# Moving the per-layer embedding from pairs 9 to 13 to pairs 2 to 6 of a mixture of experts, with 12 in place of 9 loads ahead of a branch

## The chip, the cores and the metric

The kernel runs on one core of one Trainium2 chip. The metric is the device time of one execution in microseconds (us); the time of a kernel is the median over its runs.

## What is computed

The program is two transformer blocks, one behind the other, on 512 tokens of width 1024, all in fp32. The second takes the first one's output. The change touches only the end of the first block:

```python
h = rmsnorm(x, g_ffn[i])
x = x + hier_moe(h, w_grp[i], w_exp[i], w1[i], w3[i], w2[i])
h = rmsnorm(x, g_ple[i])
x = x + jax.nn.sigmoid(h @ w_pg[i]) * (p[i] @ w_ple[i])
return rmsnorm(x, g_final)
```

`hier_moe` picks for every token one of 4 groups and two of its 8 experts, and adds for both `(silu(xb @ w1[e]) * (xb @ w3[e])) @ w2[e]`, weighted by the gates. An expert's w1 and w3 are 1024 x 512, its w2 is 512 x 1024. There is no limit to the tokens of an expert. The last but one line is the per-layer embedding: `p` is 512 x 256, `w_ple` 256 x 1024, `w_pg` 1024 x 1024. The product `p @ w_ple` depends on nothing that comes before it.

## The kernel before

**Order of the stages.** The first block's mixer, the experts, the embedding's gate (`w_pg`), then the second block's mixer and its MLP. The functions here are `moe` (L736 to L863), `Weights` (L686 to L733), `experts` (L1116 to L1270) and `Ple` (from L1274).

**Experts.** The 32 experts are worked through in 16 pairs, counted from 0. Each expert has room for 64 tokens, so that the two of a pair fill the two halves of 128 partitions. For a pair, `up` multiplies the gathered tokens by w1 and by w3 (`pa`, L1141 for one expert, L1142 for the other; 32 records each time), ScalarE (ACT) and VectorE (DVE) form the gated value `ms` (L1189 to L1191), TensorE (PE) transposes it (`pact`, L1204), ACT copies the transposes to `aT` (L1217), `second` multiplies by w2 (`py`, L1239 and L1240), ACT and DVE split the result into two parts `y`, and `back` multiplies by the dispatch matrix `OT` (`pc`, L1153), which DVE adds to the residual X (L1155). The pairs overlap: `up` with w1 of the next pair is issued ahead of the `py` of this one.

**Weights.** One pair needs 12 loads of 1 MB: four tiles each of w1, w3 and w2. `Weights` keeps a list of free slots. `next` gives the next tile and puts its slot back on the list, and `fetch` issues the load of a tile into a slot (L719, on SyncE, SP). All loads lie on the one queue of SP, which works in order, and each waits for one of eight semaphores, in turn, so that eight are outstanding. A load also waits for the readers of what lay in its slot. Of the slots, 8 are buffers of a ring (tiles `ww`), the others lie in other pools (`wr`, `we`, `wh`, `wm`, named after the pool).

**The embedding in steps.** `Ple.early` is a generator; `moe` calls its steps from hooks that `experts` runs behind `aT` of a given pair (L1218):

- At pair PLE_AT, `embed` (L826) takes 6 slots from the weights, two of pool `we` (for the result) and four of the ring. Then it loads p (`praw`, L1286, 0.5 MB) and w_ple (`wraw`, L1287, 1 MB) into ring buffers. Of 20 slots 14 are left.
- At the next pair p is transposed (8 transposes L1294) and split into two parts, w_ple too; at this and the following two pairs come 48 products `pw`.
- At PLE_AT + 4, `rest` (L830) gives the four ring buffers back: 18 slots.

```python
def embed():
    W.drop(tags[1:] + ring[:4])
    next(pl.steps)
...
steps = {PLE_AT + i: lambda: next(pl.steps, 0) for i in range(1, 4)}
steps.update({-1: where, PLE_AT: embed, PLE_AT + 4: rest})
xs, pa = experts(N, bufs, c, W, 0, 14, [d], then=steps, H=H)
```

**The branch.** Experts with more than 64 tokens are handled in a loop that runs only if there are any (L852). It stands between pairs 13 and 14. Ahead of it the kernel fetches AHEAD loads (L840) and reads the count into registers (L841) on all engines. With these inputs the loop is not entered. Behind it come the other weight loads, then the two halves of `w_pg`'s first part (`Ple.load`, L1306), g_final (L1335) and `w_pg`'s second part. The `w_pg` tiles are split for the products by ACT (L165) and DVE (L167), from `pl.start` at the end of pair 15.

**Who sets the order.** The code says what is computed; a scheduler of the framework orders the instructions of each engine when the kernel is built. Each engine then works through its own list in order.

Of the kernel before, what the change touches and what calls it, by code (L numbers as in the profile page):

```python
# [26 lines left out]
TMP = 5  # L27
LA = 0
LB = 1
PLE_AT = 9  # L30
AHEAD = 9
HI0 = 2048
NEG = -3.0e38

# [651 lines left out]
class Weights:  # L686
# [35 lines left out]
    def next(self):  # L722
        i, self.i = self.i, self.i + 1
        if i not in self.got:
            self.fetch(1, i)
        raw, slot = self.got.pop(i)
        self.free.append(slot)
        return raw
# [7 lines left out]
def moe(N, a, mg, mixed):  # L736
# [4 lines left out]
    with ExitStack() as ctx:  # L741
# [91 lines left out]
# [5 lines that stand above are left out]
        over = [s for s in W.free if s not in ring][-3:]  # L838
        W.drop(over)
        W.fetch(AHEAD)  # L840
        n = nc.values_load(more[:1, 0:1], min_val=0, max_val=7)  # L841
# [1005 lines left out]
```

## Time and profile before

| | |
|---|---|
| runs | 1790.24, 1790.33, 1791.94 us, median 1790.33 |
| profiled execution | 1791.52 us, its span 1789.7 |
| mean granted TensorE clock | 0.996 |
| TensorE busy | 1746.7 us, 98% of the span |
| VectorE, ScalarE busy | 857.4 us (48%), 578.6 us (32%) |
| moved by DMA | 322.60 MB, mean 180 GB/s |
| expert stage | about 400 to 850 us of the span |

Times of rows are microseconds from the start of the span. A row of a timeline gives an instruction's start and length, its engine and line, `out<-in` and, in brackets, the engine's idle time before it and what released it. Engine names with a q (SPq, PEq) are the sequencers, which issue the instructions. The clock is given as a share of 2.4 GHz.

### The profile page before, as it was taken

The numbers are of one execution on the slowest core, as the hardware profiler recorded it, in microseconds if no ns is written. First come the engines' busy times: TensorE is split into PE (matmuls) and PEld (weight loads), VectorE is DVE, ScalarE is ACT, GpSimd is POOL, SyncE is SP. The second block draws the span as 40 slices with busy tenths as digits, with TensorE's granted clock in tenths as the row PEclk, the third lists the DMA queues.
The fourth block names the chain that finished last, engine by engine and source line by source line (L and its number), as shares of the span: only waits on it lengthen the run. The fifth ranks groups of instructions, "written<-read, shape, count | busy, mean of one in ns | idle before, by whom it ended". The sixth has DMA issues, their size and how long they took to land.

```text
span 1789.7 us, 20888 instructions
## 1 busy us (share of the span) xinstructions
PE 1746.7 (98%) x8425; PEld 1236.4 (69%) x8425; DVE 857.4 (48%) x1604; ACT 578.6 (32%) x937; POOL 83.6 (5%) x144
## 2 busy tenths in 40 slices
PE   8999999999999998999999999999999999999998
PEld 6777888864444443443776678788888888888886
DVE  7665434465545544343855647544335433333333
ACT  5453322321111111211756742324223432222221
POOL 3001000110000000000020010000000000000000
PEclk9999999999999999999999999999999999999999
DMA  5123224879999999999211032112233133322221
GB/s 195 56 86 119 76 94 147 327 287 422 424 423 423 423 421 423 423 394 384 75 48 59 25 98 71 48 51 91 83 106 133 67 94 94 95 94 94 94 94 48
DMA packets 117888, 322.60 MB, mean 180 GB/s; under 512 B 8797, under 2 KB 69393, under 8 KB 93720
## 3 DMA queue, kind: packets, MB, share of 16 engines
q1 hardware_dynamic: 115176, 315.46, 46.3%
q0 software_dynamic: 2016, 3.64, 0.5%
q10 hardware_dynamic: 592, 2.10, 0.3%
q8 instruction: 68, 1.11, 0.3%
q14 instruction: 36, 0.29, 0.0%
HBM read 320.68 MB, written 4.19 MB: 182 GB/s over the span
## 4 chain that ended last, share of the span: by engine, by line
PE 51%; ACT 2%; DVE 1%; issue 1%; POOL 0%; DVEq 0%; POOLq 0%; ACTq 0%
PE acc L279 8%; PE acc L281 8%; PE acc L280 8%; PE pf L281 3%; PE pf L280 3%; PE pf L279 3%; PE pg L279 2%; PE pg L280 2%; PE pg L281 2%; PE psc L1671 2%; PE pu L279 1%; PE pu L280 1%; PE pu L281 1%; PE pa L1141 1%; PE py L1239 1%
## 5 line engine op out<-in xcount | busy, mean ns | idle before, releaser
L167 DVE TENSOR_TENSOR wlo<-wraw,whi 128x1024 fp32r<-128x1024 f32 (+2 forms) x165 | 225.8, 1380 | 368.8 <-PE pg L280 110.5
L165 ACT ACTIVATE whi<-wraw 128x1024 fp32r<-128x1024 f32 (+2 forms) x169 | 192.7, 1164 | 248.3 <-DMA wraw<-in_w_ff_dram 121.8
L279 PE MATMUL acc<-wh,whi 128*128 128x512 f32 (+1 forms) x432 | 164.1, 380 | 2.0 <-ACT sq L1462 1.2
L281 PE MATMUL acc<-wh,wlo 128*128 128x512 f32 (+1 forms) x432 | 163.6, 379 | 0.0
L280 PE MATMUL acc<-wh,whi 128*128 128x512 f32 (+1 forms) x432 | 163.4, 378 | 0.0
L279 PE MATMUL acc<-whi,wh 128*128 128x512 f32 x288 | 116.5, 405 | 1.5 <-ACT wh L165 1.5
L1155 DVE TENSOR_TENSOR X<-pc,X 128x512 f32<-128x512 f32 x128 | 79.6, 683 | 77.5 <-PE pc L1153 77.5
L280 PE MATMUL acc<-wlo,wh 128*128 128x512 f32 x288 | 115.4, 401 | 0.0
L281 PE MATMUL acc<-whi,wh 128*128 128x512 f32 x288 | 115.1, 401 | 0.1
L279 PE MATMUL pg<-wh,whi 128*128 128x512 f32 x256 | 101.4, 396 | 0.0
L281 PE MATMUL pg<-wh,wlo 128*128 128x512 f32 x256 | 101.3, 396 | 0.0
L280 PE MATMUL pg<-wh,whi 128*128 128x512 f32 x256 | 101.2, 395 | 0.0
L279 PE MATMUL pf<-whi,jh 128*128 128x512 f32 x256 | 101.1, 395 | 0.0
L280 PE MATMUL pf<-wlo,jh 128*128 128x512 f32 x256 | 101.1, 395 | 0.0
L281 PE MATMUL pf<-whi,jl 128*128 128x512 f32 x256 | 101.1, 395 | 0.0
L279 PEld LDWEIGHTS acc<-wh,whi 128*128 128x128 f32 x432 | 81.3, 188 | 21.1 <-ACT sq L1462 1.7
L281 PEld LDWEIGHTS acc<-wh,wlo 128*128 128x128 f32 x432 | 81.3, 188 | 17.2 <-issue 1.2
L280 PEld LDWEIGHTS acc<-wh,whi 128*128 128x128 f32 x432 | 81.3, 188 | 15.6
L1141 PE MATMUL pa<-ww,wm 128*64 128x512 f32 x176 | 79.3, 597 | 2.6 <-DVE y L169 2.2
L169 DVE SCALAR_TENSOR_TENSOR y<-py,gsl,y 128x512 fp32r<-128x512 f32 x32 | 24.0, 750 | 117.3 <-ACT y L165 116.6
L1142 PE MATMUL pa<-ww,wm 128*64 128x512 f32 x168 | 76.8, 598 | 0.0
L1153 PE MATMUL pc<-y,OT 128*128 128x512 f32 x256 | 69.4, 413 | 0.2 <-DVE X L1155 0.2
(484 smaller groups left out, 3468.7 us busy)
## 6 DMA issues: line engine op xcount, KB each, us to landing
ww<-in_w_dram SPq DMA_DIRECT2D x71, 1024.0 KB
wraw<-in_w_in_dram SPq DMA_DIRECT2D x44, 1024.0 KB
wr<-in_w_dram SPq DMA_DIRECT2D x34, 1024.0 KB
wm<-in_w_dram SPq DMA_DIRECT2D x33, 1024.0 KB
wraw<-in_w_ff_dram SPq DMA_DIRECT2D x32, 1024.0 KB
wh<-in_w_dram SPq DMA_DIRECT2D x31, 1024.0 KB
we<-in_w_dram SPq DMA_DIRECT2D x23, 1024.0 KB
wraw<-in_w_out_dram SPq DMA_DIRECT2D x8, 1024.0 KB
```

The costliest lines, as they stand in the source:

```text
L165: nc.scalar.activation(hi, src, AF.Copy, scale=scale)
L167: (pool or nc.vector).tensor_tensor(lo, src, f32v(hi), op=OP.subtract)
L169: nc.vector.scalar_tensor_tensor(lo, src, scale, f32v(hi), op0=OP.mult, op1=OP.subtract)
L279: mm(out, lhsT=lh, rhs=rh, start=start, stop=False, **kw)
L280: mm(out, lhsT=lh, rhs=rl, start=False, stop=False, **kw)
L281: self.mm = mm(out, lhsT=ll, rhs=rh, start=False, stop=stop, **kw).ins
L1141: nc.tensor.matmul(p[0:64], lhsT=x.xT[:, kk, :64], rhs=wt[0][:, k, :], start=kk == 0, stop=kk == 7)
L1142: x.ups.append(nc.tensor.matmul(p[64:128], lhsT=x.xT[:, kk, 64:], rhs=wt[1][:, k, :], start=kk == 0, stop=kk == 7).ins)
L1153: ins = nc.tensor.matmul(pc, lhsT=OT[:, t * P:(t + 1) * P], rhs=y[i], start=i == 0, stop=i == 1).ins
L1155: nc.vector.tensor_tensor(x, pc, x, op=OP.add)
L1239: nc.tensor.matmul(p[0:64], lhsT=aT[:, f, 0:64], rhs=wt[0][:, i, :], start=f == 0, stop=f == 3)
L1671: nc.tensor.matmul(pl[:, cs], lhsT=fk[:, m, cs], rhs=fq[:, m, cs], start=True, stop=True)
```

## The change

```diff
@@ -27,8 +27,8 @@
 TMP = 5
 LA = 0
 LB = 1
-PLE_AT = 9
-AHEAD = 9
+PLE_AT = 2
+AHEAD = 12
 HI0 = 2048
 NEG = -3.0e38
```

PLE_AT moves the embedding's steps from pairs 9 to 13 to pairs 2 to 6, and with them the time in which the weights have fewer slots. AHEAD puts three more loads in front of the branch.

On SP, in before, the loads of p and w_ple stand behind 120 weight loads:

```order
L719 DMA wm_4884<-in_w_dram 128x2048
L719 DMA ww<-in_w_dram 128x2048 x4
L719 DMA wr_4978<-in_w_dram 128x2048
L1286 DMA praw<-in_p_dram 128x4x256
L263 DMA wraw<-in_w_ple_dram 128x2x1024
L719 DMA wr_5027<-in_w_dram 128x2048
L719 DMA wr_5029<-in_w_dram 128x2048
```

and now behind 36, ahead of the tiles of w2 of pair 2:

```order
L719 DMA wm_3702<-in_w_dram 128x2048
L719 DMA ww<-in_w_dram 128x2048
L1286 DMA praw<-in_p_dram 128x4x256
L263 DMA wraw<-in_w_ple_dram 128x2x1024
L719 DMA wr_3753<-in_w_dram 128x2048
L719 DMA wr_3755<-in_w_dram 128x2048
```

Some loads further on SP, now, the last `ww` here is the second tile of w2 of pair 3:

```order
L719 DMA wh_3798<-in_w_dram 128x2048
L719 DMA ww<-in_w_dram 128x2048 x3
L719 DMA wm_3890<-in_w_dram 128x2048
L719 DMA wm_3892<-in_w_dram 128x2048
L719 DMA wm_3954<-in_w_dram 128x2048
L719 DMA wr_3966<-in_w_dram 128x2048
L719 DMA wr_3968<-in_w_dram 128x2048
L719 DMA wr_3987<-in_w_dram 128x2048
L719 DMA we_3989<-in_w_dram 128x2048
L719 DMA ww<-in_w_dram 128x2048
L719 DMA wh_3999<-in_w_dram 128x2048
```

It comes behind three `wr` and one `we`, which are needed later than it. In before a `ww` stands in the same way behind three `wr` and a `we`, at the tiles of w2 of pair 10.

On SP behind the branch (L841 ISA is its end), in before 11 weight loads stand ahead of w_pg:

```order
L841 ISA x2
L719 DMA wh_8942<-in_w_dram 128x2048
L719 DMA ww<-in_w_dram 128x2048 x5
L719 DMA wm_8987<-in_w_dram 128x2048
L719 DMA wm_9040<-in_w_dram 128x4x512
L719 DMA wm_9042<-in_w_dram 128x4x512
L719 DMA ww<-in_w_dram 128x4x512 x2
L263 DMA wraw<-in_w_pg_dram 128x4x512 x2
```

and now 8:

```order
L841 ISA x2
L719 DMA wr_8973<-in_w_dram 128x2048
L719 DMA ww<-in_w_dram 128x2048 x2
L719 DMA we_8987<-in_w_dram 128x2048
L719 DMA ww<-in_w_dram 128x4x512 x4
L263 DMA wraw<-in_w_pg_dram 128x4x512 x2
```

On ACT behind the branch, in before, the conversions of w_pg (`wh<-wraw`) begin behind the first `y` of pair 15:

```order
L852 UNCONDITIONAL_BRANCH x2
L1189 ACTIVATE ms<-pa,rsl 128x512
L1217 ACTIVATE aT<-pact 128x512
L165 ACTIVATE y<-py,gsl 128x512 x2
L1189 ACTIVATE ms<-pa,rsl 128x512
L1217 ACTIVATE aT<-pact 128x512
L165 ACTIVATE y<-py,gsl 128x512
L165 ACTIVATE wh_9120<-wraw 128x512
L195 ACTIVATE jk,ss<-X 128x512
```

and now four of them stand ahead of `aT` of pair 15, four more ahead of its `y`:

```order
L852 UNCONDITIONAL_BRANCH x2
L1189 ACTIVATE ms<-pa,rsl 128x512
L1217 ACTIVATE aT<-pact 128x512
L165 ACTIVATE y<-py,gsl 128x512 x2
L1189 ACTIVATE ms<-pa,rsl 128x512
L165 ACTIVATE wh_9120<-wraw 128x512 x4
L1217 ACTIVATE aT<-pact 128x512
L165 ACTIVATE wh_9201<-wraw 128x512 x4
```

## Rows read from the trace of the kernel before

**Rows 1.** The page, parts 1 and 2: engines, DMA tenths and GB/s in 40 slices.

```profile
PE 1746.7 (98%) x8425; PEld 1236.4 (69%) x8425; DVE 857.4 (48%) x1604; ACT 578.6 (32%) x937; POOL 83.6 (5%) x144
...
DMA  5123224879999999999211032112233133322221
GB/s 195 56 86 119 76 94 147 327 287 422 424 423 423 423 421 423 423 394 384 75 48 59 25 98 71 48 51 91 83 106 133 67 94 94 95 94 94 94 94 48
```

**Rows 2.** Stage table: us; busy (count) of PE, PEld, DVE, ACT, POOL; clock, DMA share, GB/s.

```profile
460.00:490.00 30.00, 30.00 (x147) 12.64 (x144) 15.88 (x47) 4.39 (x9) 1.98 (x2) 1.00 1.01 424
...
670.00:700.00 30.00, 22.94 (x101) 10.44 (x102) 13.72 (x29) 5.53 (x9) 1.06 (x1) 0.89 1.01 423
...
790.00:820.00 30.00, 28.47 (x127) 11.63 (x127) 14.46 (x28) 2.66 (x4) 0.00 (x0) 1.00 0.83 338
820.00:850.00 30.00, 27.44 (x116) 11.70 (x112) 11.24 (x18) 4.39 (x7) 0.00 (x0) 0.94 1.04 408
850.00:880.00 30.00, 29.98 (x141) 22.07 (x140) 27.88 (x56) 25.71 (x60) 3.40 (x4) 1.00 0.23 78
880.00:910.00 30.00, 28.56 (x131) 22.87 (x130) 21.55 (x45) 19.14 (x37) 2.98 (x6) 1.00 0.11 36
```

**Rows 3.** TensorE's timeline, pairs 2 and 3: start, us, line, out<-in, count.

```profile
466.97 0.59 PE L1239 MATMUL py<-ww,aT 128*64 128x512 f32 x1
...
480.94 2.12 PE L1153 MATMUL pc<-y,OT 128*128 128x512 f32 x8
...
493.61 0.59 PE L1239 MATMUL py<-ww,aT 128*64 128x512 f32 x1
```

**Rows 4.** TensorE's timeline, pairs 9 and 10; in brackets idle time before, releaser.

```profile
670.87 0.64 PE L1142 MATMUL pa<-wm,wm 128*64 128x512 f32 x1 [0.72 <-DMA wm<-in_w_dram]
...
695.02 1.11 PE L1239 MATMUL py<-ww,aT 128*64 128x512 f32 x1 [6.34 <-DMA ww<-in_w_dram]
...
699.28 0.59 PE L1239 MATMUL py<-ww,aT 128*64 128x512 f32 x1
...
699.71 0.59 PE L1239 MATMUL py<-ww,aT 128*64 128x512 f32 x1
```

**Rows 5.** SP's timeline (a DMA issue), then its waits, 660 to 710.

```profile
681.22 0.33 SPq L719 DMA_DIRECT2D ww<-in_w_dram  x1
...
SPq L719 <- PE pa L1142: 5.8, 2, 5.4
```

**Rows 6.** SP's timeline, pair 3: first issue's start, stretch of the x3 issues.

```profile
474.45 4.85 SPq L719 DMA_DIRECT2D wr<-in_w_dram  x3
```

**Rows 7.** The branch: timelines of TensorE and SP, line L852, DMA tenths 800 to 812.

```profile
807.51 0.59 PE L1141 MATMUL pa<-we,wm 128*64 128x512 f32 x1
807.52 0.59 PE L1142 MATMUL pa<-wh,wm 128*64 128x512 f32 x1
...
809.78 0.61 PE L1141 MATMUL pa<-ww,wm 128*64 128x512 f32 x1 [0.38 <-PEq L852]
...
786.83 20.36 SPq L719 DMA_DIRECT2D wh<-in_w_dram  x3
...
L852 SPq COMPARE_BRANCH  x1: 50/50/50, 793.5 to 793.5; - x1
...
L852 PEldq COMPARE_BRANCH  x1: 3366/3366/3366, 805.5 to 805.5; - x1
...
DMA  9978778555423211100001000090489999999999
```

**Rows 8.** Pair 15: timelines of TensorE, then ScalarE.

```profile
827.11 0.64 PE L1141 MATMUL pa<-ww,wm 128*64 128x512 f32 x1
...
834.13 2.14 PE L1153 MATMUL pc<-y,OT 128*128 128x512 f32 x8
838.83 0.84 PE L1204 MATMUL pact<-ident,ms 128*128 128x128 f32 x4 [2.56 <-DVE ms L1191]
839.32 3.59 PE L1153 MATMUL pc<-y,OT 128*128 128x512 f32 x8
842.84 0.64 PE L1239 MATMUL py<-wm,aT 128*64 128x512 f32 x1
...
839.70 0.60 ACT L1217 ACTIVATE aT<-pact 128x512 f32<-128x512 f32 x1 [2.94 <-PE pact L1204]
...
855.94 2.19 ACT L165 ACTIVATE wh<-wraw 128x512 fp32r<-128x512 f32 x4
```

## The prediction

> **What bounds the kernel now.** I read the page first, then the stage table, then the timelines of the engines around the places that the change touches. The page shows TensorE (PE) busy for 98% of the span, but also a band, slices 10 to 17, in which the DMA engines are full at 421 to 424 GB/s [rows 1]. That band is the expert stage, and the stage table narrows it: in every stretch that I read from 460 to 700 us the DMA share is 1.01, and only from 790 on does it fall [rows 2]. So between 430 and 790 us two things are nearly full at once. A pair of experts needs 12 loads of 1 MB; at 423 GB/s a load of 1.05 MB takes 2.48 us, so 12 take 29.8 us. TensorE needs less for a pair: it starts the products of one pair at 466.97 and of the next at 493.61, 26.6 us [rows 3]. The stream loses some 3 us of its lead per pair, and the kernel lives on the lead that it has at the start.
>
> Pairs are counted from 0, as in the code. The lead runs out at pairs 9 and 10. There TensorE waits twice for a load: 0.72 us and 6.34 us [rows 4]. The first is the lead at its end. The second is of another kind: the awaited `ww` was issued only at 681.22, after SP had waited up to 5.4 us for products (PE pa L1142) to release a ring buffer [rows 5]. It is the load that the embedding's 5 ring tiles push behind others. After that wait the granted clock is at its lower level: the five steps of products from 695.02 to 699.28 take 4.26 us, where five take 2.15 at the upper one (0.43 a step, 699.28 to 699.71) [rows 4]. The stage shows 0.89 for its mean clock [rows 2]. The three items sum to 0.72 + 6.34 + 2.1 = 9.2 us, and they are what moving the embedding could remove.
>
> **Part 1: the embedding at pairs 2 to 6.** Its own work (two loads, 8 transposes, 48 products, the splits) is the same instructions elsewhere: no term. What moves with it is the shortage of buffers: 20 weight slots become 14 for four pairs, then 18. Now the lead is largest there, so does a wait follow? The order shows one displaced load, the second tile of w2 of pair 3, behind four others. Its buffer comes free when the products with w3 of pair 3 end, 480.94 [rows 3]. A load on an idle queue takes about 4.5 us: when SP issues again at 806.86 (the last of its three `wh`, 786.83 + 20.36 - 0.33), the DMA engines are busy again from 808.4 on (slices of 0.3 us), then 2.48 for the bytes and something for completion [rows 7]. So it lands at about 485.5, and TensorE needs it at 493.61 [rows 3]: no wait, 8 us to spare. **The 9.2 us at pair 10 go.**
>
> But 14 slots hold less of a lead than 20, so the DMA engines, which ran without a pause before, now have some. Size: the displaced tile is now the 54th of the stream. SP keeps eight loads outstanding, so in before the 62nd was issued when the 54th had landed: 478.97 (the last of the three `wr`, 474.45 + 4.85 - 0.33) [rows 6]. Ahead of it there now lie p (0.5 MB) and w_ple (1 MB), 1.5 x 2.48 = 3.7 us: 482.7 if the queue never ran dry. It lands at 485.5 instead. **The stream is 2.8 us late**, call it 3. Bounds: 0 if the queue never runs dry; 8 if each of the four loads that are issued singly there cost its full 4.5 - 2.48 = 2 us. I take 3, since it comes from this place's own rows. From then on the queue is full as before, and a full queue can't catch up.
>
> What then is the 9.2 us worth? The last two loads that the branch needs, the second half of w1 of pair 15, are used at 807.51 and 807.52. Behind them SP had one more load, the last; its bytes stopped moving at 805.1 and SP resumed at 806.86, so the one before, 2.48 earlier, had landed between 802.6 and 804.4: I take 803.5, a lead of 4.0 us [rows 7]. TensorE comes 9 us earlier, waits for this same stream, and gets it 3 us later than before: 806.5 in place of 807.5. **Gain up to the branch: 1.0 us**, bounds +4.0 and -5.
>
> **Part 2: the branch.** In before, TensorE's sequencer reaches the branch at 805.5 and takes 3.37 us in it, while queued products run to 809.4: a gap of only 0.38 [rows 7]. Now the sequencer stands at products that wait for a load until 806.5; behind them only four steps are left. In before 809.78 - 805.5 - 3.37 = 0.9 us lie around those 3.37; 806.5 + 3.4 + 0.9 gives a restart at 810.8, where it was 809.78: **+1.0 us**. Bounds: -1 if the branch stays hidden, +4.5 if the code's fetch takes twice as long beside full DMA engines (in before they are idle then).
>
> **Part 3: 12 loads ahead, and who waits behind them.** SP can't pass the branch before all its loads have landed: it stood at the three `wh` for 20.36 us, and the DMA engines were idle until its next issue [rows 7]. With three more loads (7.5 us) and a stream 3 us late it resumes at 806.86 + 10.5 = 817.4. Behind it now come 8 weight loads, then w_pg, where 11 came before. The first four, w3 of pair 15, land by 817.4 + 4.5 + 3 x 2.57 = 829.6; their second half is needed in the middle between 827.11 and 834.13 [rows 8], plus the 1.0: no wait, by some 2 us. The first half of w_pg lands at 817.4 + 4.5 + 8 x 2.57 = 842.5 (1.05 MB at the 408 GB/s of 820 to 850 [rows 2]); as the queue has been some 1 us slower than its mean at other places, 842.5 to 843.5.
>
> Who waits for it is new. On ScalarE (ACT) the four conversions of this load stood behind the `y` of pair 15; the order now puts them ahead of `aT` of pair 15. In before `aT` runs at 839.70, 0.9 us after its transposes, and the products start at 842.84 [rows 8]. Now: 843 + 4 conversions, 2.2 us (four in 2.19 [rows 8]) + `aT` 0.6 + 0.3 = 846.1 to 846.6, and DVE's two subtractions of the same load stand ahead of its adds in the same way. **+3.7 us at the last products, which takes in part 2.** Bounds: +1.0 if w_pg lands by 840; +5.5 if the adds hold the matrix products back too.
>
> The Trainium skill (TensorE: Matmul & The Clock Gate, Engine queue depths) calls ACT and DVE strict FIFO. By that the `aT` must wait and the sum is this one; without it the sum would end with part 2, at +1.0. No row of before shows an instruction there that overtakes another.
>
> **Part 4: the clock.** After the 2.56 us wait at 838.83 eight matrix products take 3.59 us, where eight take 2.14 [rows 8]: the lower level already costs 1.5 there. TensorE will now wait some 4 us more right behind. After 6.34 us it cost 2.1 [rows 4]; part of it will lie inside the wait. I take **+1.0**, bounds 0 and 3.4. The same page's Terms put the penalty at throttled time x (1 - K/N), half of the time at the lower level; by that the sum would be higher by another 1, the row says less because part of that time is idle.
>
> **Part 5: given back.** The conversions are done earlier, but TensorE is busy 29.98 of the 30 us after 850; only 880 to 910 has 1.4 us of idle time [rows 2]. **-0.3**, bounds 0 and -1.4.
>
> **Sum:** +3.7 + 1.0 - 0.3 = +4.4 us. The profiled execution took 1791.52; its sum is 1795.9. The median of three runs, 1790.33, lies 1.2 lower, so for the median 1794.7; I say **1795**.
>
> **Rivals.** *The gain is kept* (faster): the stall goes and the stream has room to follow, so that all 9.2 us stay; 1790.3 - 9.2 = 1781. It needs 9 us of slack in the stream, and the lead at the branch was 4.0. A smaller version, no lost lead (+4.0) and `aT` not held, ends at about 1786. Together **0.10**.
>
> *Nothing is left of it* (no change): the stream is the limit before and after, the 9.2 us turn into a wait at pair 14 or 15, and w_pg lands by 840 or the wait for it is shared with the pause that is there already (2.56 us). Then -1 to +2: 1790 to 1792. **0.33**.
>
> *More than I count* (slower still): the stall comes back at pair 3. The point from which it decides is 8 us of delay of one load, the price 6 to 9 us taken from a stretch where the lead then still grows, so much of it would be hidden. **0.04** within the slower case.
>
> **Chances.** A measurement of this kernel tells about 0.2% (3.6 us) from no change: 1786.7 to 1793.9. Forecast and what is slower than it by the bounds of parts 2 to 4: **0.57** slower; **0.33** the same; **0.10** faster. The range takes in the no-change case to its lower half and the upper bounds (+5.5 + 3.4 + 1 = about +10): **1788.5 to 1800**. The forecast's own range is 1793 to 1800.
>
> **What would show it.** No DMA wait above 2 us between 430 and 780, and pairs of 26.6 to 28 us wherever the embedding has no work; a new wait of about 6 us for a load of w1 of pair 15 at 793 to 800, with the clock down after it; PE's branch gap above 2 us; SP's longest wait at L852 ending at about 817; `aT` of pair 15 behind four `wh<-wraw` at about 845 to 847. I am wrong if DMA share drops nowhere in 455 to 490, if the last `py` starts before 844, or if the restart behind the branch is before 809.

## The result, and the profile after

The changed kernel takes 1801.21 us in the median of 5 runs (1800.26 to 1801.98), the kernel before 1790.33 (1790.16 to 1792.42). Run against run the ratio is 1.0053, with a 95% interval of 1.0042 to 1.0064: 9.5 us slower (7.5 to 11.5). The profiled execution took 1801.21 us, its span is 1799.3, 9.6 more than before; the mean granted clock is 0.994. The direction is the one forecast. The size is twice the forecast 4.7, the median lies 1.2 us above the upper end of the range (1800), and the loss comes from another place than the one that was to carry most of it.

The stage table of the kernel after, same columns as in [rows 2]:

```profile
430.00:460.00 30.00, 30.00 (x151) 13.11 (x152) 17.16 (x45) 5.28 (x11) 0.99 (x1) 1.00 1.00 404
460.00:490.00 30.00, 30.00 (x145) 12.33 (x142) 16.33 (x51) 4.81 (x11) 1.98 (x2) 1.00 0.95 376
...
550.00:580.00 30.00, 29.27 (x126) 13.43 (x125) 9.33 (x22) 4.57 (x8) 0.87 (x1) 1.00 1.00 403
670.00:700.00 30.00, 29.27 (x141) 13.09 (x141) 15.83 (x39) 4.20 (x9) 1.06 (x1) 1.00 1.01 422
790.00:820.00 30.00, 19.53 (x57) 6.96 (x55) 9.50 (x19) 2.06 (x3) 0.00 (x0) 0.77 0.88 368
```

Two stretches of the kernel before that were not shown ahead, for comparison:

```profile
430.00:460.00 30.00, 30.00 (x151) 12.83 (x151) 17.16 (x48) 5.25 (x12) 0.99 (x1) 1.00 1.01 423
...
550.00:580.00 30.00, 29.27 (x143) 12.78 (x141) 13.84 (x36) 4.02 (x8) 1.06 (x1) 1.00 1.01 423
```

What was to go is gone: at 670 to 700 TensorE is busy for 29.27 us in place of 22.94, at the full clock. What was feared is there too. The DMA engines moved 404, 376 and 403 GB/s at 430 to 460, 460 to 490 and 550 to 580, where they moved 423 to 424: 19, 48 and 20 GB/s less for 30 us each, 2.6 MB, or 6.2 us of a stream of 423 GB/s. And nearly all of the loss is in one stretch, 790 to 820: TensorE is busy for 19.53 us of 30 (28.47 before), with a mean clock of 0.77.

TensorE's timeline of the kernel after in that stretch and at pair 15:

```profile
801.21 1.97 PE L1141 MATMUL pa<-ww,wm 128*64 128x512 f32 x2 [4.67 <-DMA ww<-in_w_dram]
804.21 1.11 PE L1142 MATMUL pa<-ww,wm 128*64 128x512 f32 x1 [1.03 <-DMA ww<-in_w_dram]
...
809.38 0.79 PE L1142 MATMUL pa<-ww,wm 128*64 128x512 f32 x1
...
810.44 0.59 PE L1142 MATMUL pa<-wm,wm 128*64 128x512 f32 x1
...
816.87 1.08 PE L1141 MATMUL pa<-ww,wm 128*64 128x512 f32 x1 [4.55 <-PEq L852]
...
817.75 1.06 PE L1141 MATMUL pa<-ww,wm 128*64 128x512 f32 x1
...
820.17 0.59 PE L1141 MATMUL pa<-ww,wm 128*64 128x512 f32 x1
...
847.44 1.11 PE L1204 MATMUL pact<-ident,ms 128*128 128x128 f32 x4 [2.57 <-DVE ms L1191]
...
851.40 0.64 PE L1239 MATMUL py<-ww,aT 128*64 128x512 f32 x1
```

SP's timeline of the kernel after around the branch (the issues of the three `wr` reach over it):

```profile
795.56 25.11 SPq L719 DMA_DIRECT2D wr<-in_w_dram  x3
820.78 0.85 SPq L719 DMA_DIRECT2D ww<-in_w_dram  x2
```

Line L852 of the kernel after (ns as min/median/max, first and last start):

```profile
L852 PEldq COMPARE_BRANCH  x1: 6146/6146/6146, 810.4 to 810.4; - x1
```

DMA tenths of the kernel after from 800 to 820, 40 slices of 0.5 us:

```profile
DMA  8999999989999999999999999998898632310000
```

SP's waits at the branch, for its eight semaphores (first and last start), of the kernel after, then of the kernel before:

```profile
L852 SPq EVENT_SEMAPHORE  x8: 17/17/17, 809.8 to 819.9; - x8
L852 SPq EVENT_SEMAPHORE  x8: 17/17/17, 803.5 to 806.4; - x8
```

TensorE stood at w1 of pair 15 for 4.67 and 1.03 us, and took its last tile (L1142, `wm`) at 810.44, where it took it at 807.52 before [rows 7]. SP passes the first of its waits there 6.3 us later than before (809.8 and 803.5), which agrees with the 6.2 us of the stream. The row of that last tile shows no wait: after the 4.67 us its clock is at the lower level, and the six steps from 804.21 to 809.38 take 5.17 us, 0.86 each, where a step at the upper level takes 0.43 [rows 4]. So about the last 0.6 us of the delay before the branch (810.44 less 809.8) are the clock's.

TensorE's sequencer reached the branch at 810.4, 4.9 us later than before (805.5), and stayed in it for 6.15 us in place of 3.37. TensorE restarts at 816.87 in place of 809.78: **+7.1 us**, 4.9 + 2.8 less 0.6 that lay around the branch before and no longer does. SP issues again at 820.78 (the forecast had 817.4), where it was 806.86. The DMA engines, nearly idle beside the branch before [rows 7], are at 8 tenths or more until 815.5 now.

Then the clock is down: the step from 816.87 to 817.75 takes 0.88 where one at the upper level takes 0.43 [rows 4], and the four steps up to 820.17 take 3.3 us in place of 1.7, some 1.6 more. The last products start at 851.40 in place of 842.84 [rows 8], +8.6. The remaining microsecond of the 9.6 lies behind, and I did not locate it.

ACT's timeline of the kernel after at pair 15:

```profile
846.85 2.19 ACT L165 ACTIVATE wh<-wraw 128x512 fp32r<-128x512 f32 x4 [1.48 <-DMA wraw<-in_w_pg_dram]
848.95 0.57 ACT L1217 ACTIVATE aT<-pact 128x512 f32<-128x512 f32 x1
```

The conversions of w_pg do stand ahead of `aT`, as in the order, and ACT waits 1.48 us for the load. But TensorE's transposes (`pact`) come only at 847.44, and `aT` at 848.95. From the transposes to the last products it is 4.0 us as before (851.40 - 847.44 here, 842.84 - 838.83 in [rows 8]): this wait costs nothing here.

### The profile page after: what moved, and what is told of

Read it like the earlier page. It is cut to its first block, busy times and chain, and to the rows that moved or that the text cites. A ratio compares the mean times of both kernels' runs of the same rounds, so it can differ in the third digit from the quotient of the medians.

```text
span 1799.3 us, 20889 instructions
## 1 busy us (share of the span) xinstructions
PE 1752.2 (97%) x8425; PEld 1237.9 (69%) x8425; DVE 858.0 (48%) x1604; ACT 578.6 (32%) x937; POOL 83.5 (5%) x144
## 4 chain that ended last, share of the span: by engine, by line
PE 50%; ACT 2%; DVE 2%; issue 1%; POOL 0%; DVEq 0%; POOLq 0%; ACTq 0%
PE acc L279 8%; PE acc L281 8%; PE acc L280 8%; PE pf L281 3%; PE pf L280 3%; PE pf L279 3%; PE pg L281 2%; PE pg L279 2%; PE pg L280 2%; PE psc L1671 2%; PE pu L281 1%; PE pu L279 1%; PE pu L280 1%; PE pa L1141 1%; PE py L1239 1%
## 5 line engine op out<-in xcount | busy, mean ns | idle before, releaser
L1142 PE MATMUL pa<-ww,wm 128*64 128x512 f32 x232 | 109.4, 617 | 1.5 <-DMA ww<-in_w_dram 1.5
L1141 PE MATMUL pa<-ww,wm 128*64 128x512 f32 x152 | 74.4, 634 | 10.7 <-DMA ww<-in_w_dram 4.7
```

Source lines behind the costliest of these rows:

```text
L1141: nc.tensor.matmul(p[0:64], lhsT=x.xT[:, kk, :64], rhs=wt[0][:, k, :], start=kk == 0, stop=kk == 7)
L1142: x.ups.append(nc.tensor.matmul(p[64:128], lhsT=x.xT[:, kk, 64:], rhs=wt[1][:, k, :], start=kk == 0, stop=kk == 7).ins)
```

## The experiments

Two questions were open. Is the branch's length a matter of the DMA engines? And is the late stream a matter of the slots? All ratios are against runs of the kernel before on the same chip.

**1. The embedding early, 9 loads ahead.**

```diff
-PLE_AT = 9
+PLE_AT = 2
 AHEAD = 9
```

> The embedding at pairs 2 to 6 as in the change, but 9 loads ahead of the branch as before. Theory A (the branch's code fetch queues behind the weight loads that are still on the DMA engines): the stream is as late as in the change (TensorE waits for w1 of pair 15 until about 801, reaches the branch at about 810.4), but hardly a load is left beside the fetch, so the branch takes 3.4 to 4.5 us in place of 6.15 and the restart comes at 814 to 815.2; the time is 1.7 to 2.8 us below the changed kernel's, 1797 to 1799 for a before of 1790. Rival B (6.15 us is what a branch costs that TensorE reaches with nothing queued, whatever the DMA engines do): 6.1 us, restart 816.9, time as the change, 1800 to 1801. Rival C (the conversions of w_pg ahead of aT cost 3 us, as the prediction had it): they stand behind aT here, so more than 3 us below the change even with a branch of 6 us.

1796.39 us, ratio 1.0024 (1.0015 to 1.0034). Line L852 of this run, then the restart in TensorE's timeline:

```profile
L852 PEldq COMPARE_BRANCH  x1: 3352/3352/3352, 809.8 to 809.8; - x1
```

```profile
813.50 0.78 PE L1141 MATMUL pa<-ww,wm 128*64 128x512 f32 x1 [2.34 <-PEq L852]
```

TensorE reaches the branch at 809.8, 0.6 us before the change does, and is through in 3.35 us: theory A, and not B. Three loads less beside the branch are worth 3.4 us at the restart (813.50 against 816.87), those 0.6 and 2.8 of the branch. Rival C's 3 us are not there: from the restart to the last products it takes 34.7 us in this run (they start at 848.25) and 34.5 in the change. But by the ratios the time is some 5 us below the change's, where theory A had 1.7 to 2.8; the rest of it lies behind pair 15 and was not located.

**2. The embedding late, 12 loads ahead.**

```diff
 PLE_AT = 9
-AHEAD = 9
+AHEAD = 12
```

> The embedding at pairs 9 to 13 as before, but 12 loads ahead of the branch. Theory A: nothing changes up to the branch (stall of 6.3 us at pair 10, branch reached at 805.5), then the fetch queues behind three loads and the branch takes about 6 us: restart at about 812, 2 to 3 us later than before; the conversions of w_pg stand ahead of aT but w_pg lands by 840. Time 2 to 4 us above before, 1792 to 1794. Rival B (the branch's length does not depend on the DMA engines): 3.4 us, restart 809.8, no change, 1789.5 to 1791.

1796.54 us, ratio 1.0026 (1.0016 to 1.0036), a little more than theory A had. Line L852 of this run:

```profile
L852 PEldq COMPARE_BRANCH  x1: 4832/4832/4832, 805.8 to 805.8; - x1
```

TensorE's timeline of this run, restart and pair 15, then ACT's:

```profile
811.16 0.61 PE L1141 MATMUL pa<-ww,wm 128*64 128x512 f32 x1 [1.54 <-DVEq L852]
...
840.20 0.66 PE L1204 MATMUL pact<-ident,ms 128*128 128x128 f32 x4 [2.57 <-DVE ms L1191]
...
846.14 1.11 PE L1153 MATMUL pc<-y,OT 128*128 128x512 f32 x2 [3.89 <-ACT aT L1217]
847.18 1.12 PE L1239 MATMUL py<-wm,aT 128*64 128x512 f32 x1
```

```profile
843.41 2.19 ACT L165 ACTIVATE wh<-wraw 128x512 fp32r<-128x512 f32 x4 [5.29 <-DMA wraw<-in_w_pg_dram]
845.51 0.57 ACT L1217 ACTIVATE aT<-pact 128x512 f32<-128x512 f32 x1
```

The branch takes 4.83 us with the embedding where it was, so it is the loads beside it that lengthen it. That is only 1.4 us at the restart (811.16 against 809.78). The larger part stands at pair 15: here TensorE is early enough for part 3 of the prediction. ACT waits for w_pg until 843.41, converts for 2.2 us, and `aT` follows at 845.51; TensorE waits 3.89 us for it, and the last products start at 847.18, 4.3 us later than before. My expectation said that w_pg would land by 840; that was wrong, and with it the size.

**3. The embedding at pairs 5 to 9, 9 loads ahead** (`PLE_AT = 5`).

> The embedding at pairs 5 to 9, 9 loads ahead. Theory: the loss of the stream comes from having 14 slots while the lead is long; at pair 5 the lead is still some 20 us, so a walk through the queue by hand has the DMA engines idle once for about 5 us around 572 and TensorE waiting some 2 to 3 us at pair 6, the last loads of w1 of pair 15 5 us later than before, and a branch of 3.4 to 4.5 us: 1795 to 1799. Rival (the loss is made by pairs 2 to 4 alone): a stream on time, 1789 to 1791.

1797.98 us, ratio 1.0035 (1.0020 to 1.0049). Stage table of this run, then TensorE's timeline:

```profile
550.00:580.00 30.00, 27.34 (x130) 11.93 (x128) 17.16 (x39) 6.90 (x11) 1.06 (x1) 1.00 0.78 319
```

```profile
579.26 0.64 PE L1240 MATMUL py<-ww,aT 128*64 128x512 f32 x1 [1.94 <-DMA ww<-in_w_dram]
...
814.10 0.61 PE L1141 MATMUL pa<-ww,wm 128*64 128x512 f32 x1 [2.09 <-PEq L852]
```

The stream pauses at the new place, 319 GB/s in place of 423, 7.4 us; TensorE waits for the displaced load there, and the restart is at 814.10. It reaches the branch at 810.4, just when the change does, and with 9 loads ahead takes 3.37 us there. The pairs 2 to 4 are no exception.

**4. The embedding at pairs 7 to 11, 9 loads ahead** (`PLE_AT = 7`).

> The embedding at pairs 7 to 11, 9 loads ahead. Theory: here 14 slots hold the lead that is left, so the DMA engines do not run dry, and the displaced load is still early enough (a wait of 1 to 2 us in place of 6.3 at pair 8). The stream is on time, TensorE waits about 2 us for w1 of pair 15 and reaches the branch at about 805, the restart is at 809 to 809.8: most of the 9.2 us that go at pair 10 are lost to the stream and to the branch, -1 to +0.5 us, 1789 to 1791. Rival (the stream has room): 4 to 9 us faster, 1781 to 1786.

1791.57 us, ratio 0.9997 (0.9987 to 1.0006). Stage table of this run, then TensorE's timeline:

```profile
550.00:580.00 30.00, 29.27 (x142) 12.88 (x139) 13.84 (x36) 4.03 (x8) 1.06 (x1) 1.00 1.01 423
```

```profile
804.83 0.64 PE L1142 MATMUL pa<-ww,wm 128*64 128x512 f32 x1 [1.74 <-SPq L852]
...
809.61 1.08 PE L1141 MATMUL pa<-wr,wm 128*64 128x512 f32 x1 [2.85 <-PEq L852]
```

With the lead down to what 14 slots can hold, the stream does not pause. The stall of 6.34 us is gone, and the time is the same: TensorE waits 1.74 us for the second half of w1 of pair 15 instead (the row names SP at L852; SP stands there for the same loads, one after the other from 804.8 on, when TensorE goes on), and 2.85 us at the branch, which is no longer hidden. That is 4.2 of the 9.2 us, with the 0.38 at the branch before taken off. At the transposes of pair 13 TensorE is 5.4 us ahead of the kernel before (782.59 against 788.03), so the other 3.8 are lost ahead of it; I did not take them apart in this run.

**5. Late, 12 loads ahead, conversions behind.** As experiment 2, and with the conversions of w_pg on ACT, and DVE's subtractions of the same load, held behind `aT` of pair 15:

```diff
-        nc.scalar.activation(aT, pt.rearrange("p (f s) -> p f s", f=4), AF.Copy)
+        turned = nc.scalar.activation(aT, pt.rearrange("p (f s) -> p f s", f=4), AF.Copy).ins
...
-                    then.get(pi + 1, int)()
+                    with tc.issue_after(turned):
+                        then.get(pi + 1, int)()
```

> As the run with the embedding late and 12 loads ahead, but the conversions of w_pg are held behind aT of pair 15 on ACT and behind the adds on DVE. Theory: there aT waited for them and for the w_pg load (3.89 us on TensorE behind aT, last products 4.3 us later than before, of which 1.4 from the branch); with them behind, the last products start at about 844.2 and only the branch's 1.4 us and a little are left: 0.5 to 2.5 us above before. Rival (the wait is for w_pg's bytes, whatever the order): as that run, 4 to 5.5 us above before.

1792.89 us, ratio 1.0006 (0.9996 to 1.0015). TensorE's timeline of this run:

```profile
840.58 0.66 PE L1204 MATMUL pact<-ident,ms 128*128 128x128 f32 x4 [2.58 <-DVE ms L1191]
...
843.01 0.64 PE L1239 MATMUL py<-wm,aT 128*64 128x512 f32 x1
```

From the transposes to the last products it is 2.4 us, and the wait for `aT` is gone. The last products start 4.2 us earlier than in experiment 2 (843.01 against 847.18), though the restart is 0.4 later: that is what the order cost there. That the time is level with before is in part the clock: the branch still takes 5.05 us and the restart is 1.8 us later than before (811.54), but the eight products behind the transposes take 2.09 us in place of 3.59 [rows 8], at a mean clock from 820 to 850 of 1.00 in place of 0.94 [rows 2]. Why the clock did not fall here was not tested.

**6. The change, conversions behind.** The same edit on the changed kernel.

> The change with the conversions of w_pg held behind aT of pair 15. Theory: in the change the restart behind the branch is so late (816.9) that w_pg has landed by then and aT waits 0.6 us for the conversions at most; so no difference: within 1 us of the change, 9 to 11 us above before. Rival (the prediction's part 3: this order is the main loss): 3 us or more below the change.

1800.82 us, ratio 1.0046 (1.0029 to 1.0062), which overlaps the change's own. TensorE's timeline of this run:

```profile
815.77 1.08 PE L1141 MATMUL pa<-ww,wm 128*64 128x512 f32 x1 [5.01 <-PEq L852]
...
851.10 1.12 PE L1239 MATMUL py<-ww,aT 128*64 128x512 f32 x1
```

The gap at the branch is there (5.01 us), and the last products start at 851.10, where they start at 851.40 in the change. The edit that took 4.2 us off experiment 2 brings the change 0.3 us there, and no gain in time that four runs can tell.

**7. Only the slots.** The embedding late and 9 loads ahead, as before; six slots are withheld from pair 2 to pair 6, and no other work is moved. (The change gives four of its six back at pair 6, here it is all six.)

```diff
+        held = tags[1:] + ring[:4]
+        steps[2] = lambda: W.drop(held)
+        steps[6] = lambda: W.free.extend(held)
         xs, pa = experts(N, bufs, c, W, 0, 14, [d], then=steps, H=H)
```

> The kernel before with the embedding where it was, at pairs 9 to 13, and 9 loads ahead; only the six weight slots are taken away at pair 2 and given back at pair 6, with no load or product moved. Theory (14 slots at a long lead make the DMA engines run dry): the DMA share falls below 1 between 450 and 490, the stream is 4 to 6 us late from then on, the lead ends one or two pairs earlier, the last load of w1 of pair 15 lands at 808 to 810 and the restart is 4 to 5 us later than before: 4 to 6.5 us above before. Rival (the lateness comes from the 1.5 MB of p and w_ple going first): the DMA share stays at 1.01, within 1 us of before.

1798.07 us, ratio 1.0031 (1.0019 to 1.0044). Stage table of this run, then TensorE's timeline (this kernel's lines are three higher, L1144 is L1141):

```profile
430.00:460.00 30.00, 30.00 (x151) 12.81 (x151) 17.17 (x48) 5.09 (x12) 0.99 (x1) 1.00 0.91 355
460.00:490.00 30.00, 30.00 (x147) 12.62 (x143) 15.78 (x47) 4.46 (x10) 1.98 (x2) 1.00 0.97 395
```

```profile
817.00 0.61 PE L1144 MATMUL pa<-wr,wm 128*64 128x512 f32 x1 [0.31 <-PEq L855]
```

355 and 395 GB/s in place of 423 and 424: 2.9 MB, 6.9 us, without p or w_ple in the stream at that place. So the slots by themselves make the stream late. All of the loss lies ahead of 490 here; from 550 to 580 this run moves 423 GB/s, so the change's 20 GB/s less there are not explained by it. The restart is at 817.00, 7.2 us late (4 to 5 were expected), and the branch is hidden but for 0.31 us. TensorE met the late loads at pairs 9 and 10, with seven waits of 0.36 to 1.28 us between 643 and 701: at the transposes of pair 10 it is 6.0 us later than before (689.18 against 683.19). The rest came in among the embedding's products, and I did not take it apart.

**8. The embedding at pairs 8 to 12, 9 loads ahead** (`PLE_AT = 8`).

> The embedding at pairs 8 to 12, 9 loads ahead. A walk through the queue finds no pause of the DMA engines and no wait of TensorE for a displaced load, and the stream on time: TensorE reaches the branch 1 to 2 us earlier than before and the restart is at 807.8 to 809.5: 0 to 2 us below before. Rival (a gain of the whole 9 us): 6 us or more below.

1791.29 us, ratio 0.9997 (0.9987 to 1.0007). TensorE's waits in this run from 430 to 790 (us in total, times, longest), then in the kernel before:

```profile
PE pa L1141 <- DVE y L169: 6.5, 9, 0.7
PE pw L279 <- ACT we L1304: 2.7, 4, 0.7
```

```profile
PE pa L1141 <- DVE y L169: 5.1, 7, 0.7
```

TensorE's timeline of this run around pairs 9 and 10, and the restart:

```profile
659.20 0.64 PE L1239 MATMUL py<-wh,aT 128*64 128x512 f32 x1
...
673.70 1.02 PE L1142 MATMUL pa<-ww,wm 128*64 128x512 f32 x2
...
675.31 1.07 PE L1141 MATMUL pa<-ww,wm 128*64 128x512 f32 x2
...
765.31 0.59 PE L1239 MATMUL py<-ww,aT 128*64 128x512 f32 x1
...
810.16 0.61 PE L1141 MATMUL pa<-ww,wm 128*64 128x512 f32 x1 [0.31 <-PEq L852]
```

The same two products in the kernel before:

```profile
657.84 0.59 PE L1239 MATMUL py<-wr,aT 128*64 128x512 f32 x1
...
764.85 0.64 PE L1239 MATMUL py<-wm,aT 128*64 128x512 f32 x1
```

No wait for a load is left between 430 and 790, and still TensorE is not earlier at the branch. From the products with w2 of pair 9 to those of pair 12 it is 106.1 us (659.20 to 765.31), in before 107.0 with the stall (657.84 to 764.85): 0.9 us gained of 9.2. Two things in the rows took part of the rest. The scheduler has put the same 48 products `pw` among the experts' products in another way, with waits for copies of ACT (2.7 us) and 1.4 us more of waits for `y` on DVE. And it splits partners: L1141 and L1142 use half of the array each and run beside each other, two in a step of 0.43 us, but at 673.70 and 675.31 two of one line follow each other with no partner: four steps for what takes two. From 430 to 790 there are 12 such rows, 6 in before; 6 more rows of two lone steps cost 6 x 0.43 = 2.6 us. That makes 6.7 of 8.3; the remaining 1.6 I did not find. So my walk through the queue, which took the embedding's work as costing the same anywhere, failed here, and no version beat the kernel before.

## Why the prediction was right, and where it was short

*Pair 10 (part 1): right.* The 9.2 us of stall and lower clock went; TensorE started the products of pair 13 at 784.57 in place of 792.32, 7.8 us earlier where the text had 9. No wait came at pair 3, where the text had 8 us to spare.

*The lead lost by 14 slots (part 1): right in kind, and the larger of the two terms that failed in size.* "The stream is 2.8 us late, call it 3" was worked out at one tile, the 54th. The stage tables show 6.2 us. My walk ended at that tile, but the slots are short for four pairs, and about a quarter of the loss, at 550 to 580 (20 of 87 GB/s), came behind it. Experiment 7 shows that slots alone do it, 6.9 us, but not the part at 550 to 580, whose cause stays open. So "a gain up to the branch of 1.0" became a loss: the last tile of w1 of pair 15 was taken at 810.44 and not at 806.5; a lead of 4.0 less 6.2 gives +2.2, and 810.44 is +2.9; the 0.7 between them go to the lower clock ahead of the branch, which the text did not have.

*The branch (part 2): this is the step that failed,* by its own term and by the late stream that it took over. "+1.0 us" at the restart, with an upper bound of +4.5, measured +7.1. The restart comes 6.1 us after the forecast 810.8. Of these, 3.9 are the sequencer's arrival (810.4, where the text had 806.5), which is the stream term above with the clock; 2.8 are the branch (6.15 for 3.37); 0.6 come off, the time around it. For the branch the text took the 3.37 us of before as they were, though it names the code's fetch beside full DMA engines and has twice as long as its bound. The measured 6.15 us lie inside that bound; the sum leaves it because the late stream comes on top. I should have taken the longer value: of 12 loads ahead, four stand behind the last one that TensorE needs for the branch, so they are still under way there.

*w_pg ahead of aT (part 3): right in mechanism, no term here.* It was the largest term, +3.7 "which takes in part 2". Experiment 2 shows it at work, 3.89 us, and experiment 5 takes it away. But the two waits don't add, the later one ends last, and with the branch 7 us late the conversions were no longer it (experiment 6). The Trainium skill's strict FIFO (TensorE: Matmul & The Clock Gate, Engine queue depths) agrees with experiment 2's rows, where `aT` starts at 845.51, as the conversions ahead of it end (843.41 + 2.19).

*The clock (part 4): +1.0 forecast, about 1.6 measured,* behind the branch and not behind the wait for w_pg. *Given back (part 5):* nothing that can be seen.

*The rivals.* That all is kept, or that nothing is left of it, both fell. "Nothing is left of it" describes experiments 4 and 8, where the stream does not pause.

*The total.* That the direction came out is in part luck. Of the forecast +4.4, +3.7 hung on the conversions ahead of `aT`, and in the change they cost nothing; the slowdown was carried by the stream and the branch, for which the text had +1.0 together.

The parts of the change, apart: the embedding early costs 0.24%, the 12 loads 0.26% by themselves, together 0.53%. That looks like a plain sum, but it isn't one: the 12 loads cost 3.9 us by the order on ACT when alone, and by the longer branch when the embedding is early.

## What to carry to other kernels

A stall that stands in front of a saturated stream is not worth its length: ask first how far ahead the stream is at the next place that needs it (here 4.0 us of 9.2), and whether the buffers that the cure takes away shorten that lead. Work that borrows prefetch buffers does not slow the stream where the lead is no longer than the buffers that remain can hold; experiments 4 and 8 did that, and were as fast as before, not faster. Price a branch at the length that it has with loads under way beside it (here 4.8 to 6.2 us, not 3.4), and of several late waits take the one that ends last rather than their sum.

## What was not expected of the hardware

The branch's length on TensorE went with the loads under way beside it: 3.35 to 3.87 us in the runs with 9 loads ahead (3.37 before), 4.83 and 5.05 with 12 ahead and the embedding late, 6.15 and 6.19 with 12 ahead and the embedding early. The compare-and-branch itself took 50 ns on SP [rows 7].

Data queue (q1: packets, MB, share of 16 engines) while TensorE's sequencer is in the branch, kernel after from 810 to 817, then experiment 1 from 809.5 to 813.5:

```profile
q1 hardware_dynamic: 343, 2.44, 83.6%
```

```profile
q1 hardware_dynamic: 10, 0.06, 3.5%
```

While TensorE is in the branch, each run moves one packet of an instruction queue (q8). Here it is in the kernel after, stretch 814.0 to 814.1, then in experiment 1, stretch 810.8 to 810.9:

```profile
q8 instruction: 1, 0.02, 67.9%
```

```profile
q8 instruction: 1, 0.02, 59.1%
```

The same for seven of the kernels, in stretches of 0.1 us (us from the start of the span; the last column is what the DMA engines moved while TensorE was in the branch):

| run | loads ahead | branch starts | packet | branch ends | GB/s |
|---|---|---|---|---|---|
| before | 9 | 805.5 | 806.5 | 808.9 | 61 |
| experiment 1 | 9 | 809.8 | 810.8 | 813.2 | 17 |
| experiment 4 | 9 | 805.4 | 806.9 | 809.3 | 19 |
| experiment 2 | 12 | 805.8 | 808.1 | 810.6 | 324 |
| experiment 5 | 12 | 805.9 | 808.4 | 811.0 | 318 |
| after | 12 | 810.4 | 814.0 | 816.5 | 365 |
| experiment 6 | 12 | 809.2 | 812.9 | 815.4 | 369 |

From the packet to the end of the branch it is 2.4 to 2.7 us in all ten kernels. From the start of the branch to the packet it is 1.0 to 1.5 us with 9 loads ahead, 2.3 and 2.5 with 12 and the embedding late, 3.6 and 3.7 with 12 and the embedding early. So nearly all that the branch grows by lies in front of this packet, in the runs in which the engines are full of data. That the packet carries the code behind the branch, and that it waits behind the data, is how I read it; no run showed the packet's own issue.
